# Turning the memory of a cross attention early, through a DRAM scratch, in a hybrid mLSTM/HGRN2 block

## The chip, the cores and the metric

The kernel runs on one core of a Trainium2 chip. The metric is the device time of one execution in microseconds, as a median of several runs. The core has five engines that matter here: TensorE (PE in the profile, its weight loads PEld), VectorE (DVE), ScalarE (ACT), GpSimd (POOL) and SyncE (SP), which issues most of the DMAs. Each engine takes its own instructions in the order in which the program lists them; semaphores make one wait for another.

## The reference

One block of a network in float32, batch 1, 256 tokens, width 2048: a feed-forward stage, a mixer of two recurrences, a cross attention over a memory of 256 rows, and a second feed-forward stage, each added to the residual stream.

```python
for l in range(DEPTH):
    h = rmsnorm(x, norm_ffn1[l])
    x = x + 0.5 * swiglu(h, ffn1_w1[l], ffn1_w3[l], ffn1_w2[l])
...
    h = rmsnorm(x, norm_xattn[l])
    m = rmsnorm(mem, norm_mem[l])
    x = x + cross_attention(h, m, xattn_wq[l], xattn_wkv[l], xattn_wo[l])
    h = rmsnorm(x, norm_ffn2[l])
    x = x + 0.5 * swiglu(h, ffn2_w1[l], ffn2_w3[l], ffn2_w2[l])
return rmsnorm(x, norm_final)
```

`mem` has 256 rows of 2048. Its norm divides each row by its root mean square and multiplies each column by `norm_mem`. `xattn_wkv` (2048 x 4096) then makes keys and values of four heads from it. The mixer is left out here, since the change does not touch it.

## The kernel before

**Gemms.** A matrix product has the activations as stationary operand and the weights streaming past. An activation of 256 rows is held turned: the 2048 columns lie on the partitions, in four chunks of 512 columns, each a tile of 128 x 4 x 256. Every float32 operand is split in two parts of lower precision, a high part (`oh` for activations, `wh` for weights) and the rest (`ol`, `wl`); a product is three matmuls, high by high (L269), high activation by low weight (L270) and low activation by high weight (L271).

A weight matrix is cut into units of four blocks of 128 rows by 512 columns, 1 MB, loaded by one DMA of SP into one of four raw buffers (`wr`). A unit is used in two pieces (four in the very first). For each piece `split` makes the high part with a copy on ScalarE (`wh`, L210) and the rest with a subtraction on VectorE (`wl`, L211); both have four buffers. A piece is twelve matmuls: two row blocks of weights, two halves of 128 tokens, three matmuls each.

**Order.** `run` goes through the pieces one after another: it emits loads for the pieces up to seven ahead, splits up to three ahead, then the matmuls of the piece, and calls `tick`. `tick` runs work that was put off: things due after a number of ticks (`after`), and a background list `self.bg`, from which it takes up to three items a tick as long as the estimated backlog of VectorE and ScalarE is under 2 us. The names `pa` are accumulators of gemms (four), `ps` other PSUM tiles (four). The framework's scheduler then places each engine's instructions, and may move them against the order of emission.

**First feed-forward stage.** For each of eleven columns of 512, a gemm with `ffn1_w1` (evicted by ScalarE with a Silu into `sil`) and one with `ffn1_w3` (multiplied into `sil` by VectorE, the "products"), eight pieces each. The products are then turned on VectorE: `turned` issues 16 transposes of 32 partitions by 256 elements, which turn every 32x32 block and put it at its place (`tt`); the copy `oh` and the rest `ol` follow.

**The memory.** After the first of four query gemms of the cross attention, `mem_prep` puts the memory's work into the background list: it loads four chunks of 256 x 512 (`mem`, two tiles of 128 rows each), sums their squares on ScalarE (`memss`), and turns them with `turn` on TensorE: a matmul with the identity for each block of 128 x 128 (L299), 32 in all, from where ScalarE and VectorE evict them as `oh` and `ol`, multiplied by `norm_mem`. The row factor `memr`, from the squares, is applied later, to keys and values. All tiles of 4 KB a partition (`mem`, `sil`, `tt`, `oh`, `ol` and others) share one pool `s4` of 22 buffers.

Instructions on VectorE and ScalarE pass through a small class that adds up their estimated time, so that all of them have line 90 in the profile; there one goes by the names of the tiles.

Of the kernel before, what the change touches and what calls it, by code (L numbers as in the profile page):

```python
# [12 lines left out]
F32 = mybir.dt.float32  # L13
F32R = mybir.dt.float32r
AF = mybir.ActivationFunctionType
ALU = mybir.AluOpType
# [3 lines left out]
P = 128  # L20
T = 256
D = 2048
# [39 lines left out]
class Sub:  # L62
    def __init__(self, unit, index, mm):
        self.unit, self.index, self.mm = unit, index, mm
        self.hi = self.lo = None
# [40 lines left out]
class Block:  # L106
# [4 lines left out]
    def __init__(self, ctx, tc, a, out):  # L111
        self.tc, self.nc, self.a, self.out = tc, Core(tc.nc), a, out
        pool = lambda name, bufs, **kw: ctx.enter_context(tc.tile_pool(name=name, bufs=bufs, **kw))
        self.const = pool("const", 1)
        self.xp = pool("xp", 1)
        self.wraw = pool("wraw", 4)
        self.whi = pool("whi", 4)
        self.wlo = pool("wlo", 4)
        self.s4 = pool("s4", 22)
        self.s2 = pool("s2", 4)  # L120
        self.small = pool("small", 4)
        self.acc = pool("acc", 4, space=PSUM)
        self.tr = pool("tr", 4, space=PSUM)
        self.steps = []
        self.now = 0
        self.pe = self.ready = 0.0
        self.unwritten = {}
        self.timed = []
        self.bg = deque()
        self.uid = 0  # L130
# [354 lines left out]
            if c < 3:  # L485
                self.load(units[c], parts=2 if c == 0 else 1)

    def rstd_of(self, ss, n, dim):
        nc = self.nc
        ms = self.sm(n, "ms")  # L490
        nc.vector.tensor_scalar(ms, ss, 1.0 / dim, EPS, op0=ALU.mult, op1=ALU.add)
        r = self.sm(n, "rstd", tag=f"rstd{n}")
        nc.gpsimd.tensor_tensor(r, ms, self.mhalf[:, :n], op=ALU.pow)
        nc.vector.end += 0.9
        return r
# [484 lines left out]
        return ths  # L980


    def mem_prep(self):
        nc = self.nc
        mem, self.memT = [None] * 4, [None] * 4
        ss = self.small.tile([P, 2, 4], F32, name="memss", tag="memss", bufs=1)

        def ld(c):
            mem[c] = self.t4([P, 2, 512], name="mem")
            nc.sync.dma_start(mem[c], self.a["mem"][0][:, c * 512:(c + 1) * 512].rearrange("(t p) n -> p t n", p=P))  # L990

        def sq(c):
            for t in range(2):
                self.squares(mem[c][:, t, :], ss[:, t, c:c + 1])
            if c == 3:
                s = self.sm(2, "mst")
                nc.vector.tensor_reduce(s, ss, axis=AX.X, op=ALU.add)
                self.memr = self.rstd_of(s, 2, D)

        def tn(c, half):  # L1000
            if half == 0:
                self.memT[c] = self.pair()
            self.turn(lambda t: mem[c][:, t, :], self.col["norm_mem"][:, 4 * c:4 * c + 4], self.memT[c], (half,))

        ths = [lambda: ld(0), lambda: ld(1)]
        for c in range(4):
            ths += [lambda c=c: sq(c), lambda c=c: tn(c, 0), lambda c=c: tn(c, 1)]
            if c < 2:
                ths.append(lambda c=c: ld(c + 2))
        return ths  # L1010
# [122 lines left out]
    def build(self):  # L1133
        nc, a = self.nc, self.a
        N = {}

        def begin(name):
            if name not in N:
                N[name] = self.norm_begin(name if name != "final" else None)
            return N[name]  # L1140
# [3 lines left out]
        def first(turn_gains):  # L1144
            self.warm(9)
            self.load_x()
            n = begin("norm_ffn1")
            n.ops = [self.pair() for _ in range(4)]
            src = lambda c: (lambda t: self.x[c][:, t, :])
            pin = self.tc.keep_in_program_order  # L1150
            turn_gains()
            first_subs = [st for st in self.steps if isinstance(st, Sub)][:4]
            for k in range(4):
                self.turn_piece(src(0), n.gain, n.ops[0], k, pin)
                if k == 0:
                    self.warm(4)
                self.split(first_subs[k])
            for i in range(2, 8):
                c, h = i // 2, i % 2
                fn = lambda c=c, h=h: self.turn(src(c), n.gain[:, 4 * c:4 * c + 4], n.ops[c], (h,), pin)  # L1160
                self.after((1, 2, 4, 5, 6, 7)[i - 2], fn)
            for c in range(4):
                self.after((5, 6, 8, 9)[c], lambda c=c: self.squares_of(n, c, pin=pin))
# [58 lines left out]
        n = len(self.steps)  # L1222
        self.steps.insert(n - 60, gains)
        first(turn_gains)
        self.run()


# [34 lines left out]
```

## Time and profile before

| | us |
|---|---|
| median of 3 runs (2537.36 to 2537.74) | 2537.58 |
| the profiled execution | 2537.33 |
| its span, first to last instruction | 2535.5 |
| TensorE busy | 2525.5 |
| VectorE busy | 1729.4 |
| ScalarE busy | 1209.6 |
| matmuls of 128 x 512 by each of the three lines, mean | 0.389 to 0.391 |
| low part of a weight piece, 128 x 1024, on VectorE, mean | 1.222 |
| high part of it on ScalarE, mean | 1.052 |
| weight load of 1 MB, from issue to landing, median | 5.2 |

In a row of the profile stand the line, the engine, the operation, the tiles as output<-inputs with their shapes, the count, then busy time and the mean of one, then how long the engine was idle just before these instructions and who ended that. A row of the timeline has the start and the length in microseconds first; several like instructions in a row are merged and counted. Matmuls overlap: the next starts before the one ahead has ended, so that the time between starts tells what one costs.

The span in forty slices of 63 us, the busy share of each in tenths. The first feed-forward stage fills the slices up to the eleventh:

```profile
PE   9999999999999999999999999999999999999998
...
DVE  6666644767768877867678787677766674457665
ACT  6444434444456566574444554444544443344443
```

### The profile page before, as it was taken

What the parts mean: (1) busy time and instruction counts of PE and PEld (TensorE: products, weight loads), DVE (VectorE), ACT (ScalarE), POOL (GpSimd) and SP (SyncE); (2) the same over time, 40 slices, a digit from 0 to 9 for tenths busy, and PEclk for the clock granted to TensorE, in tenths of its full rate; (3) what the DMA queues carried; (4) which work ended last, traced back from release to release, by engine and by line L of the source; (5) the groups of instructions that cost most, each with busy time, mean ns of one, the idle gap of its engine ahead of it and who ended that gap; (6) DMA issues with size and microseconds to landing.
All of it is one profiled execution on the core that took longest, in us unless ns stands there. A gap on an engine that the chain in (4) does not pass through costs nothing.

```text
span 2535.5 us, 29137 instructions
## 1 busy us (share of the span) xinstructions
PE 2525.5 (100%) x11463; PEld 2106.1 (83%) x11463; DVE 1729.4 (68%) x2372; ACT 1209.6 (48%) x1415; POOL 14.5 (1%) x21
## 2 busy tenths in 40 slices
PE   9999999999999999999999999999999999999998
PEld 7888888888888898888888888888888888888887
DVE  6666644767768877867678787677766674457665
ACT  6444434444456566574444554444544443344443
POOL 0000000000000000000000000000000000000000
PEclk9999999999999999999999999999999999999999
DMA  8566556565555545554655665555665655655653
GB/s 279 185 197 199 188 193 198 184 199 189 194 187 186 188 138 184 176 188 166 199 192 190 207 205 169 170 174 172 194 197 191 199 191 191 198 189 193 216 189 126
DMA packets 243593, 479.92 MB, mean 189 GB/s; under 512 B 8040, under 2 KB 14976, under 8 KB 243456
## 3 DMA queue, kind: packets, MB, share of 16 engines
q1 hardware_dynamic: 242992, 476.95, 58.0%
q8 instruction: 89, 1.46, 0.2%
q10 hardware_dynamic: 464, 1.12, 0.2%
q14 instruction: 48, 0.39, 0.0%
HBM read 475.94 MB, written 2.10 MB: 189 GB/s over the span
## 4 chain that ended last, share of the span: by engine, by line
PE 98%; DVE 0%; ACT 0%; issue 0%; DMA 0%; SPq 0%; POOLq 0%; POOL 0%; DVEq 0%; ACTq 0%
PE pa L270 32%; PE pa L269 32%; PE pa L271 32%; PE ps L783 1%; PE ps L1023 0%; PE ps L1024 0%; PE ps L1022 0%; PE ps L299 0%; DVE wl L90 0%; ACT wh L90 0%; DMA wr<-in_ffn_w 0%; ACT junk L90 0%; PE ps L1097 0%; DVE ol L90 0%; DVE x L90 0%
## 5 line engine op out<-in xcount | busy, mean ns | idle before, releaser
L90 DVE TENSOR_TENSOR wl<-wr,wh 128x1024 fp32r<-128x1024 f32 (+2 forms) x906 | 1093.8, 1211 | 701.7 <-ACT wh L90 694.2
L90 ACT CAST wh<-wr 128x1024 fp32r<-128x1024 f32 (+2 forms) x906 | 942.0, 1043 | 1121.8 <-PE pa L271 1075.6
L269 PE MATMUL pa<-wh,oh 128*128 128x512 f32 (+1 forms) x3614 | 1405.8, 389 | 0.1
L270 PE MATMUL pa<-wl,oh 128*128 128x512 f32 (+1 forms) x3614 | 1400.3, 388 | 0.2 <-DVE wl L90 0.2
L271 PE MATMUL pa<-wh,ol 128*128 128x512 f32 (+1 forms) x3614 | 1399.9, 387 | 0.0
L271 PEld LDWEIGHTS pa<-wh,ol 128*128 128x128 f32 x3614 | 678.3, 188 | 137.7
L270 PEld LDWEIGHTS pa<-wl,oh 128*128 128x128 f32 x3614 | 678.5, 188 | 136.4 <-DVE wl L90 1.5
L269 PEld LDWEIGHTS pa<-wh,oh 128*128 128x128 f32 x3614 | 678.3, 188 | 136.0 <-ACT wh L90 0.3
L90 DVE STREAM_TRANSPOSE tt<-sil 32x256 f32<-32x256 f32 x352 | 153.6, 436 | 6.8
L90 DVE STREAM_TRANSPOSE tt<-x 32x256 f32<-32x256 f32 x144 | 62.8, 436 | 2.8
L90 ACT CAST oh<-tt 128x1024 fp32r<-128x1024 f32 x29 | 30.6, 1056 | 41.2 <-DVE tt L90 41.2
L90 ACT ACT_TABLE_LOAD x35 | 44.9, 1283 | 8.2 <-DVE rs L90 2.7
L90 ACT ACTIVATE oh<-tt,cols 128x256 fp32r<-128x256 f32 x52 | 23.5, 501 | 42.8 <-DVE tt L90 42.8
L90 ACT ACTIVATE sil<-pa,rstd 128x512 f32<-128x512 f32 x44 | 29.8, 689 | 18.1 <-PE pa L271 18.0
L90 DVE TENSOR_TENSOR ol<-tt,oh 128x1024 fp32r<-128x1024 f32 x29 | 35.3, 1218 | 0.2 <-PE pa L270 0.2
L90 ACT ACTIVATE oh<-ps,cols 128x256 fp32r<-128x256 f32 x44 | 20.7, 472 | 26.0 <-DVE ol L90 22.1
L90 DVE STREAM_TRANSPOSE tt<-kn 32x256 f32<-32x256 f32 x64 | 27.9, 436 | 5.6 <-ACT kn L90 4.5
L90 DVE SCALAR_TENSOR_TENSOR sil<-pa,rstd,sil 128x512 f32<-128x512 f32 x44 | 31.0, 743 | 0.3 <-PE pa L271 0.3
L90 DVE STREAM_TRANSPOSE qt<-qn 32x256 f32<-32x256 f32 x64 | 27.9, 436 | 3.4 <-ACT qn L90 2.3
L90 DVE SCALAR_TENSOR_TENSOR ol<-ps,cols,oh 128x256 fp32r<-128x256 f32 x44 | 21.0, 480 | 11.6 <-ACT oh L90 11.6
L90 ACT ACTIVATE junk<-x 128x512 f32<-128x512 f32 (+1 forms) x41 | 25.0, 612 | 7.0 <-DVE x L90 7.0
L90 DVE COPY_PREDICATED at<-cst,ps 128x128 f32<-128x128 int32 x80 | 22.7, 328 | 6.9 <-PE ps L783 6.2
(189 smaller groups left out, 668.0 us busy)
## 6 DMA issues: line engine op xcount, KB each, us to landing
wr<-in_ffn_w SPq DMA_DIRECT2D x263, 1024.0 KB, 5.2
wr<-in_w_in SPq DMA_DIRECT2D x80, 1024.0 KB, 5.0
wr<-in_xattn_wkv SPq DMA_DIRECT2D x32, 1024.0 KB, 5.4
wr<-in_w_out SPq DMA_DIRECT2D x16, 1024.0 KB, 5.0
wr<-in_xattn_wq SPq DMA_DIRECT2D x16, 1024.0 KB, 5.1
wr<-in_xattn_wo SPq DMA_DIRECT2D x16, 1024.0 KB, 5.1
wr<-in_w_in SPq DMA_DIRECT2D x12, 688.0 KB, 4.0
wr<-in_w_proj_h SPq DMA_DIRECT2D x8, 1024.0 KB, 5.3
```

The source lines that it names most:

```text
L90: return fn(out, *args, **kw)
L269: nc.tensor.matmul(o, a_h, hi[:, j, :], start=(kt == 0), stop=False)
L270: nc.tensor.matmul(o, a_h, lo[:, j, :], start=False, stop=False)
L271: nc.tensor.matmul(o, a_l, hi[:, j, :], start=False, stop=(kt == end - 1))
L783: nc.tensor.matmul(ps[:, i, :], kt[:, g, j * P:(j + 1) * P], S["qc"][:, 2 * g + j, :], start=True, stop=True)
```

## The change

The memory's work is cut in two. `mem_early` is put into the background list after 24 ticks, in the first feed-forward stage. It loads the memory, sums the squares and computes `memr`, which gets a buffer of its own. Each chunk is turned within its 32x32 blocks by two transposes on VectorE of 128 x 512 (into `mu`), and stored with four DMAs of SP into a DRAM scratch `memD`, in such an order that it can be read back turned: each store takes 32 partitions, as 1024 runs of 32 elements (128 bytes). `mem_prep`, at its old place, loads the four chunks from the scratch (`memt`, one run of 1024 elements a partition) and makes `oh` and `ol` from them on ScalarE and VectorE. The 32 matmuls with the identity are gone.

```diff
@@
-    def rstd_of(self, ss, n, dim):
+    def rstd_of(self, ss, n, dim, **kw):
         nc = self.nc
         ms = self.sm(n, "ms")
         nc.vector.tensor_scalar(ms, ss, 1.0 / dim, EPS, op0=ALU.mult, op1=ALU.add)
-        r = self.sm(n, "rstd", tag=f"rstd{n}")
+        r = self.sm(n, "rstd", **(kw or {"tag": f"rstd{n}"}))
@@
-    def mem_prep(self):
+    def mem_early(self):
         nc = self.nc
-        mem, self.memT = [None] * 4, [None] * 4
+        mem = [None] * 4
         ss = self.small.tile([P, 2, 4], F32, name="memss", tag="memss", bufs=1)
+        self.memD = self.dram.tile([4, 32, 4, 8, 4, 32], F32, name="memD")
...
             if c == 3:
                 s = self.sm(2, "mst")
                 nc.vector.tensor_reduce(s, ss, axis=AX.X, op=ALU.add)
-                self.memr = self.rstd_of(s, 2, D)
-
-        def tn(c, half):
-            if half == 0:
-                self.memT[c] = self.pair()
-            self.turn(lambda t: mem[c][:, t, :], self.col["norm_mem"][:, 4 * c:4 * c + 4], self.memT[c], (half,))
+                self.memr = self.rstd_of(s, 2, D, tag="memr", bufs=1)
+
+        def tn(c):
+            u = self.t4([P, 4, 4, 2, 32], name="mu")
+            for t in range(2):
+                nc.vector.transpose(u[:, :, :, t, :].rearrange("p j k r -> p k j r"),
+                                    mem[c][:, t, :].rearrange("p (k j c) -> p k j c", k=4, j=4))
+            for i in range(4):
+                nc.sync.dma_start(self.memD[c][:, :, :, i, :].rearrange("c j e r -> c (j e) r"),
+                                  u[32 * i:32 * i + 32].rearrange("c j k t r -> c (j k t) r"))
 
         ths = [lambda: ld(0), lambda: ld(1)]
         for c in range(4):
-            ths += [lambda c=c: sq(c), lambda c=c: tn(c, 0), lambda c=c: tn(c, 1)]
+            ths += [lambda c=c: sq(c), lambda c=c: tn(c)]
+            if c < 2:
+                ths.append(lambda c=c: ld(c + 2))
+        return ths
+
+    def mem_prep(self):
+        nc = self.nc
+        mem, self.memT = [None] * 4, [None] * 4
+
+        def ld(c):
+            mem[c] = self.t4([P, 4, T], name="memt")
+            nc.sync.dma_start(mem[c].rearrange("p k t -> p (k t)"),
+                              self.memD[c].rearrange("c j e i r -> j c (e i r)"))
+
+        def parts(c):
+            self.memT[c] = hi, lo = self.pair()
+            self.unwritten.pop(id(self.memT[c]))
+            for k in range(4):
+                g = self.col["norm_mem"][:, 4 * c + k:4 * c + k + 1]
+                nc.scalar.activation(hi[:, k, :], mem[c][:, k, :], AF.Copy, scale=g)
+                nc.vector.scalar_tensor_tensor(lo[:, k, :], in0=mem[c][:, k, :], scalar=g,
+                                               in1=hi[:, k, :].bitcast(F32), op0=ALU.mult, op1=ALU.subtract)
...
@@ build
         first(turn_gains)
+        self.after(24, lambda: self.bg.extend(self.mem_early()))
         self.run()
```

The lines of the two kernels differ by one from L124 on, and by 34 at the end. How the scheduler places the early work is seen in the order of the built programs. The buffers' numbers differ between the two kernels; the raw tiles wr_714, wr_753, wr_787 and wr_821 of before hold the same weights as wr_726, wr_791, wr_849 and wr_883 now.

SP's queue in the second pair of gemms of the first stage, before:

```order
L198 DMA wr_678<-in_ffn_w 128x4x512
L198 DMA wr_714<-in_ffn_w 128x4x512
L198 DMA wr_753<-in_ffn_w 128x4x512
L198 DMA wr_787<-in_ffn_w 128x4x512
L198 DMA wr_821<-in_ffn_w 128x4x512
```

and now, where "x4" is four stores of one chunk:

```order
L199 DMA wr_680<-in_ffn_w 128x4x512
L994 DMA mem_718<-in_mem 128x2x512
L994 DMA mem_720<-in_mem 128x2x512
L199 DMA wr_726<-in_ffn_w 128x4x512
L1010 DMA memD<-mu_744 1024x1x32 x4
L994 DMA mem_751<-in_mem 128x2x512
L1010 DMA memD<-mu_778 1024x1x32 x4
L994 DMA mem_785<-in_mem 128x2x512
L199 DMA wr_791<-in_ffn_w 128x4x512
L1010 DMA memD<-mu_809 1024x1x32 x4
L1010 DMA memD<-mu_842 1024x1x32 x4
L199 DMA wr_849<-in_ffn_w 128x4x512
```

The load of wr_791 now stands behind the stores of the second chunk (mu_778), and that of wr_849 behind those of the third and the fourth (mu_809, mu_842).

VectorE around the products of the second pair (`sil` from `pa`), before. Pieces 33 to 37 of the kernel's gemms, counted from 0, have the low parts wl_806, wl_824, wl_840, wl_858 and wl_878; the products need the end of piece 33:

```order
L90 TENSOR_TENSOR wl_806<-wr_714,wh_805 128x1024
L90 TENSOR_TENSOR wl_824<-wr_753,wh_823 128x1024
L90 TENSOR_TENSOR wl_840<-wr_753,wh_839 128x1024
L90 TENSOR_TENSOR wl_858<-wr_787,wh_857 128x1024
L90 SCALAR_TENSOR_TENSOR sil_732<-pa_739,rstd_375,sil_732 128x512
L90 SCALAR_TENSOR_TENSOR sil_732<-pa_740,rstd_375,sil_732 128x512
L90 STREAM_TRANSPOSE tt_895<-sil_732 32x2x4x32
L90 TENSOR_TENSOR wl_878<-wr_787,wh_877 128x1024
```

and now, from the low part of piece 33 (wl_868) on:

```order
L90 TENSOR_TENSOR wl_868<-wr_726,wh_867 128x1024
L90 SCALAR_TENSOR_TENSOR sil_757<-pa_764,rstd_377,sil_757 128x512
L90 SCALAR_TENSOR_TENSOR sil_757<-pa_765,rstd_377,sil_757 128x512
L90 STREAM_TRANSPOSE mu_809<-mem_751 128x4x4x32 x2
L90 STREAM_TRANSPOSE mu_842<-mem_785 128x4x4x32 x2
L90 STREAM_TRANSPOSE tt_957<-sil_757 32x2x4x32
L90 TENSOR_REDUCE mst_820<-memss 128x2
L90 STREAM_TRANSPOSE tt_957<-sil_757 32x2x4x32
L90 TENSOR_SCALAR ms_822<-mst_820 128x2
L90 STREAM_TRANSPOSE tt_957<-sil_757 32x2x4x32 x7
```

followed by

```order
L90 TENSOR_TENSOR wl_886<-wr_791,wh_885 128x1024
L90 TENSOR_TENSOR wl_902<-wr_791,wh_901 128x1024
L90 STREAM_TRANSPOSE tt_957<-sil_757 32x2x4x32 x7
L90 TENSOR_TENSOR ol_938<-tt_957,oh_937 128x1024
L90 TENSOR_TENSOR wl_920<-wr_849,wh_919 128x1024
```

The low parts of pieces 34 to 36 (wl_886, wl_902, wl_920) stood ahead of the products and stand now behind them, behind two chunks of the memory, and behind nine (piece 34) or all sixteen (piece 36) of the transposes of the products. On TensorE the new order of piece 34 has two matmuls with the high part ahead of the first with the low part, where one stood.

More of the change, by code (lines that the diff above doesn't have):

```diff
@@ L123, in __init__ @@
         self.tr = pool("tr", 4, space=PSUM)
+        self.dram = pool("dram", 1, space=bass.MemoryType.DRAM)
         self.steps = []
@@ L997, in sq @@
                 nc.vector.tensor_reduce(s, ss, axis=AX.X, op=ALU.add)
-                self.memr = self.rstd_of(s, 2, D)
-        def tn(c, half):
-            if half == 0:
-                self.memT[c] = self.pair()
-            self.turn(lambda t: mem[c][:, t, :], self.col["norm_mem"][:, 4 * c:4 * c + 4], self.memT[c], (half,))
+                self.memr = self.rstd_of(s, 2, D, tag="memr", bufs=1)
[7 more added lines that the diff above has]
+                                  u[32 * i:32 * i + 32].rearrange("c j k t r -> c (j k t) r"))
         ths = [lambda: ld(0), lambda: ld(1)]
         for c in range(4):
-            ths += [lambda c=c: sq(c), lambda c=c: tn(c, 0), lambda c=c: tn(c, 1)]
+            ths += [lambda c=c: sq(c), lambda c=c: tn(c)]
[17 more added lines that the diff above has]
+                                               in1=hi[:, k, :].bitcast(F32), op0=ALU.mult, op1=ALU.subtract)
+        ths = [lambda: ld(0), lambda: ld(1)]
+        for c in range(4):
+            ths.append(lambda c=c: parts(c))
             if c < 2:
```

## The prediction

> **What bounds the kernel now.** I read the page first: the span, the busy times, the slices and the chain.
>
> ```profile
> span 2535.5 us, 29137 instructions
> PE 2525.5 (100%) x11463; PEld 2106.1 (83%) x11463; DVE 1729.4 (68%) x2372; ACT 1209.6 (48%) x1415; POOL 14.5 (1%) x21
> ...
> PE 98%; DVE 0%; ACT 0%; issue 0%; DMA 0%; SPq 0%; POOLq 0%; POOL 0%; DVEq 0%; ACTq 0%
> ```
>
> TensorE is never without work: it is busy for 2525.5 of 2535.5 us and makes 98% of the chain. So a change gains what it takes off TensorE, and loses what TensorE then has to wait. Next the waits, of TensorE and of SP's queue.
>
> ```profile
> PE pa L270 <- DVE wl L90: 0.2, 1, 0.2
> ...
> SPq L198 <- DVE wl L90: 2080.3, 410, 9.5
> ```
>
> TensorE waits for a split weight tile once, for 0.2 us; SP, which loads the weights, sits almost all the time at a wait for a free buffer. There is room, but it is held by the order in which SP and VectorE work: both take their instructions one after another.
>
> **What goes: 32 turns on TensorE.** The memory's turns, and TensorE around two groups of them:
>
> ```profile
> L299 PE MATMUL ps<-cst,mem x32: 270/272/273, 1465.0 to 1514.9; 128*128 128x128 f32 x32
> ```
>
> ```profile
> 1459.80 0.39 PE L270 MATMUL pa<-wl,oh 128*128 128x512 f32 x1
> ...
> 1462.52 0.39 PE L270 MATMUL pa<-wl,oh 128*128 128x512 f32 x1
> ...
> 1465.02 0.60 PE L299 MATMUL ps<-cst,mem 128*128 128x128 f32 x4
> 1465.37 0.48 PE L269 MATMUL pa<-wh,oh 128*128 128x512 f32 x1
> ...
> 1468.23 0.60 PE L299 MATMUL ps<-cst,mem 128*128 128x128 f32 x4
> ```
>
> Their durations overlap, so starts count. Undisturbed, twelve matmuls go from 1459.80 to 1462.52: 2.72 us, 0.227 each. From one group of four turns to the next, 1465.02 to 1468.23, lie the four and twelve matmuls: 3.21 us. A group costs 0.49, the eight groups 3.9 us. The evictions (16 on ScalarE, 16 on VectorE) stay, from SBUF now; the eight squares and the row statistics move to the first stage. TensorE doesn't wait here now, so no more than **3.9 us** is to be had.
>
> **What comes, and where it lies.**
>
> ```profile
> L90 ACT ACTIVATE kn<-pa,rstd x8: 688/690/690, 1541.8 to 1692.5; 128x512 f32<-128x512 f32 x8
> ```
>
> Eight turns on VectorE, eight squares on ScalarE and 16 stores, four loads come into the second pair of gemms of the first feed-forward stage; the four loads back stand in the cross attention where four loads of the same size stood, and I cost them at nothing: the first key product is evicted at 1541.8, so its gemm of eight pieces starts near 1520, 49 us after the last such load goes out now (1471.2, in the row of mem loads below). VectorE is idle for 32% of the span by the page, which would hide all of the early work; the order does not let it. A gemm piece is twelve matmuls, 2.72 us, and the split runs at most four pieces ahead. I number the pieces from 0; piece 34 is the first of the third pair (wl_824 before, wl_886 now), piece 36 the one with wl_858 and wl_920.
>
> ```profile
> 92.68 1.23 DVE L90 TENSOR_TENSOR wl<-wr,wh 128x1024 fp32r<-128x1024 f32 x1 [1.49 <-ACT wh L90]
> ...
> 99.26 1.40 DVE L90 SCALAR_TENSOR_TENSOR sil<-pa,rstd,sil 128x512 f32<-128x512 f32 x2
> 100.70 0.43 DVE L90 STREAM_TRANSPOSE tt<-sil 32x256 f32<-32x256 f32 x1
> ...
> 105.34 2.23 DVE L90 STREAM_TRANSPOSE tt<-sil 32x256 f32<-32x256 f32 x5
> ...
> 112.86 1.23 DVE L90 TENSOR_TENSOR wl<-wr,wh 128x1024 fp32r<-128x1024 f32 x1
> 114.01 1.22 DVE L90 TENSOR_TENSOR ol<-tt,oh 128x1024 fp32r<-128x1024 f32 x1
> ```
>
> ```profile
> 99.78 0.39 PE L270 MATMUL pa<-wl,oh 128*128 128x512 f32 x1
> ```
>
> ```profile
> 105.22 0.39 PE L270 MATMUL pa<-wl,oh 128*128 128x512 f32 x1
> ```
>
> Before, VectorE writes the low part of piece 34 at 92.68, six microseconds before the products at 99.26, which wait for the end of piece 33. Now that low part stands behind those products, behind four memory turns and behind nine turns of the products. TensorE, which needs it at 99.78, is made to wait for all of that: piece 33, products, turns, split, piece 34, one after another. What each takes:
>
> ```profile
> L90 DVE TENSOR_TENSOR suf<-suf,pre 128x512 f32<-128x512 f32 x14 | 9.7, 689 | 1.5 <-ACT pre L90 1.4
> L90 DVE TENSOR_TENSOR at<-ps,cst 128x256 f32<-128x256 f32 x8 | 3.4, 434 | 1.7 <-PE ps L783 1.7
> L90 DVE STREAM_TRANSPOSE tt<-sil 32x256 f32<-32x256 f32 x352 | 153.6, 436 | 6.8
> ```
>
> ```profile
> 112.87 1.06 ACT L90 CAST oh<-tt 128x1024 fp32r<-128x1024 f32 x1 [1.18 <-DVE tt L90]
> ```
>
> ```profile
> L90 DVE TENSOR_REDUCE mst<-memss x1: 161/161/161, 1489.2 to 1489.2; 128x2 f32<-128x8 f32 x1
> L90 DVE TENSOR_SCALAR ms<-mst x1: 168/168/168, 1489.4 to 1489.4; 128x2 f32<-128x2 f32 x1
> ```
>
> A turn of 128x512 isn't in the trace. One of 32x256 takes 436 ns, as 256 elements a partition take in a sum (434), so I take 0.70 for 512 (689 in a sum, and a gap). Its ends are 0.44 (no more than the 32x256) and 3.5 (32x32 blocks one by one, 64 for 8); the 689 is nearest. Then: products done and next start 100.70; four memory turns 2.8, 103.5; nine turns at 2.23/5, 4.0, and the two small ones 0.35: 107.85; low part 1.22: **109.1**. TensorE goes on there.
>
> The second wait follows: low part of piece 35 until 110.2 (1.15 after the last, as 112.86 to 114.01), seven turns 3.1 to 113.35, the high part of the turned products on ScalarE 1.06 to 114.4 (VectorE's next instruction waits for it), their low part 1.22 to 115.65, wl_920 1.2 to **116.9**. TensorE, from 109.1, would be there at 114.5 (24 matmuls of 0.227); in the old run it is there at 105.22, or 105.45 in the new order with two high-part matmuls ahead. All later work moves by 116.9 - 105.45 = **11.45 us**. After that the split catches up (1.2 a piece against 2.72), and nothing gives the delay back.
>
> SP must not be later than this. Its load for pieces 34 and 35 (wr_791) stands behind the stores of the second chunk, that for 36 and 37 (wr_849) behind those of the third and fourth.
>
> ```profile
> wr<-in_ffn_w SPq DMA_DIRECT2D x263, 1024.0 KB, 5.2
> ...
> mem<-in_mem SPq DMA_DIRECT2D x4, 512.0 KB, 6.0
> ```
>
> ```profile
> L990 SPq DMA_DIRECT2D mem<-in_mem x4: 463/500/501, 1449.0 to 1471.2; - x4
> ```
>
> ```profile
> 87.24 1.22 DVE L90 TENSOR_TENSOR wl<-wr,wh 128x1024 fp32r<-128x1024 f32 x1 [1.50 <-ACT wh L90]
> ```
>
> The second chunk is turned behind the low part of 87.24: 88.5 to 89.9. Four stores at 0.5 us of SP, a memory load, the weights at 92.4: landed by 97.6, by 100.5 with the stores' own time ahead; the split needs them at 106.8. The memory load, too, lands before its turn at 102.1. The other eight stores go out from 102.1 to 106.1, wr_849 at 106.1: landed at 111.3, at 113.2 with the stores' time. Needed at 114.4: **covered by 1.2 us**, if a store's packet is cheap. A store has 1024 packets of 128 bytes, 64 for each of 16 engines. No such packet is in the trace; two windows of SP's queue, with 16-byte packets alone and with stores of 1024 bytes, bound it:
>
> ```profile
> DMA packets 58, 0.00 MB, mean 2 GB/s; under 512 B 58, under 2 KB 58, under 8 KB 58
> ...
> q1 hardware_dynamic: 58, 0.00, 4.7%
> ```
>
> ```profile
> DMA packets 319, 0.33 MB, mean 271 GB/s; under 512 B 32, under 2 KB 288, under 8 KB 319
> ...
> q1 hardware_dynamic: 319, 0.33, 77.8%
> ```
>
> The first window is 0.55 us: 0.047 x 16 x 0.55 / 58 = 7 ns of an engine, and 9.5 ns apart on the queue as a whole. The second is 1.2 us: 0.778 x 16 x 1.2 / 319 = 47 ns. Between the two by bytes, 128 give 11.5 ns, which I take, as 16 is the nearer row: the eight stores are 8 x 64 x 11.5 = 5.9 us of an engine. From 14 ns on the weights land last.
>
> ScalarE's part, and TensorE's clock:
>
> ```profile
> 91.59 1.05 ACT L90 CAST wh<-wr 128x1024 fp32r<-128x1024 f32 x1 [1.67 <-PE pa L271]
> ```
>
> ```profile
> L90 ACT ACTIVATE junk<-mem x8: 617/632/665, 1456.3 to 1478.2; 128x512 f32<-128x512 f32 x8
> L90 ACT ACTIVATION_READ_ACCUMULATOR junk<-mem x8: 186/188/224, 1456.8 to 1478.7; 128x1 f32 x8
> ```
>
> ```profile
> 2527.00:2530.80 3.80, 0.00 (x0) 0.00 (x0) 2.54 (x9) 2.14 (x6) 0.66 (x1) 1.00 0.51 190
> 2530.80:2535.00 4.20, 0.00 (x0) 0.00 (x0) 0.15 (x1) 0.00 (x0) 0.00 (x0) 0.50 0.68 250
> ```
>
> ScalarE waits 1.67 us in every piece for TensorE; a square is 0.63 and 0.19, and the four late ones are over before VectorE's nine turns are, so they cost nothing. After the last matmul the granted clock stays at 1.00 for 3.8 us and is 0.50 from then on. The wait up to 109.1 is some 8 us, so TensorE may come back at half speed. If that lasts as long, it costs half of 3.8, 1.9 us, and arrives at piece 36 at 116.4 instead of 114.5: still before 116.9, so nothing. The Trainium skill (TensorE: Matmul & The Clock Gate, Part 1: The HAM clock gate) puts the change at an idle or busy window of about 3.4 us; the rows above agree for the way down.
>
> **The sum.** Profiled execution 2537.33 (span 2535.5 and 1.8 around it), 0.25 under the median of 2537.58. 2537.33 - 3.9 + 11.45 = 2544.9, as a median **2545.1**, slower by 0.3%. With turns of 0.44: 2544; with stores at 47 ns: below.
>
> **The rivals.**
> Dear stores. At 47 ns a chunk's four stores take 12 us of an engine: they end at 103.1, the memory load behind them lands at 105.7 instead of before 102.1 (3.6 later), the eight stores take 24 us from 107.1 to 131.1, wr_849 lands at 135.1, TensorE has piece 36 at 137.4: 32 us late, 2565.7. For it: a load has to go through the same queue behind them. Against: the 16-byte row. The Trainium skill (DMA: Bandwidth & Descriptors, Specifications) says that below 512 bytes the engine reads, modifies and writes; no run here shows it yet. Twice the 11.5 ns for that would be, as an estimate by this page, 2549.5.
> A queue that can't make packets faster than 9.5 ns each: a store 9.7 us, twelve of them in the two waits 117, together some 113 late: 2647. Against: 319 packets in 1.2 us are 3.8 ns apart.
> Other side: the cover holds. All added work fits into the idle time of VectorE, wl_886 is there when piece 33 ends, as wl_824 was; then only the 3.9 are left: 2533.7, faster. It decides at one point: the low part of piece 34 would have to be done before 99.78. Against it stands the row order: products that need the end of piece 33 stand ahead of it.
> The turns cost TensorE more than I read: matmul and weight load one after another, 0.272 and 0.140, for 32 are 13.2; then 2535.8, no difference. Against: the starts above.
>
> ```profile
> L299 PEld LDWEIGHTS ps<-cst,mem x32: 138/140/143, 1464.8 to 1514.8; 128*128 128x128 f32 x32
> ```
>
> The change may also not do what it says (the memory still turned on TensorE); the row order has no such matmul left, so I give it nothing.
>
> **Chances.** Forecast (2543 to 2547) 0.55; dear stores (2547 to 2566) 0.27; slow queue 0.06; cover holds 0.07; dear turns 0.05. The low end is the cheap turn less a microsecond, the high end the 47 ns; that holds 0.82. A measurement of this kernel tells some 0.2% (5 us) from no change: faster 0.07, same 0.05, slower 0.88.
>
> **What would show it.** In the profile after: no matmul at the cross attention's line 299 with mem, and there 3.9 us less; one wait of TensorE for wl of some 9 us near 100 us, a second of 2 near 115 (longer, and for a weight load, if stores are dear); a granted clock under 1 for some microseconds behind the first; turns of 128x512 near 0.7. I am wrong if TensorE doesn't wait there, or waits anywhere else.

## The result, and the profile after

| | us |
|---|---|
| median before (5 runs, 2537.36 to 2537.74) | 2537.6 |
| median after (5 runs, 2554.29 to 2556.6) | 2555.4 |
| ratio, 95% interval | 1.007, 1.006 to 1.0081 |
| profiled execution after, its span | 2556.6, 2554.8 |

The change makes the kernel 17.8 us slower; the forecast was 7.6 slower, with 2566 as the upper end. Of all executions reported here one, of pool_st at 2594.19 us, was slow, with a granted clock of 0.926 where the others have 0.99 or more; the ratios leave it out. The page of the changed kernel first: span, busy times, and the shares of the chain that ended last, by engine.

```profile
span 2554.8 us, 29095 instructions
...
PE 2530.5 (99%) x11431; PEld 2107.7 (82%) x11431; DVE 1733.6 (68%) x2380; ACT 1209.1 (47%) x1415; POOL 13.6 (1%) x21
...
PE 96%; DMA 1%; DVE 1%; ACT 1%; issue 0%; SPq 0%; POOLq 0%; POOL 0%; ACTq 0%; DVEq 0%
```

TensorE has 32 matmuls fewer (11431 against 11463), so the turns are gone, yet it is busy for 5.0 us more, and DMA, VectorE and ScalarE have each a per cent of the chain that TensorE had. Now TensorE's waits (who, for whom, us in total, times, longest):

```profile
PE pa L271 <- DVE wl L90: 7.9, 6, 5.5
...
PE pa L270 <- ACT wh L90: 5.7, 4, 2.4
```

Ten waits for split weights, where there was one. To see where, I compared the start of every gemm matmul (`pa`, 10854 of them in both kernels) with that of the same matmul before. This table gives, for each stretch of the program, by how many microseconds the kernel loses on the old one; it serves for all runs below.

| kernel | first gemm's start | pieces up to 36 of the first stage | cross attention, turns and readback | all the rest |
|---|---|---|---|---|
| changed | +1.9 | +12.8 | +3.7 | +0.6 |
| read16 | +0.3 | +15.4 | -3.7 | +0.5 |
| early_only | +0.2 | +12.6 | 0.0 | +0.3 |
| late_4 | +0.2 | 0.0 | +3.7 | +0.6 |
| spread | +1.6 | 0.0 | +2.2 | +0.4 |
| spread16 | +0.5 | 0.0 | -3.7 | +0.4 |
| turns_only | +0.3 | 0.0 | 0.0 | +0.6 |
| stores_only | +0.3 | +13.6 | 0.0 | +0.5 |
| pool_st | +0.1 | 0.0 | 0.0 | +0.5 |
| pinned | +0.4 | +9.7 | 0.0 | +0.5 |
| pool16 | +0.2 | 0.0 | -3.7 | +0.6 |
| read2 | +0.5 | 0.0 | +24.9 | +0.5 |

The changed kernel loses in two places. **First stage.** TensorE's matmuls with an idle time ahead of them, in the timeline from 100 to 126 us:

```profile
104.04 0.73 PE L270 MATMUL pa<-wh,oh 128*128 128x512 f32 x2 [2.41 <-ACT wh L90]
110.31 0.80 PE L271 MATMUL pa<-wl,oh 128*128 128x512 f32 x1 [5.54 <-DVE wl L90]
118.71 0.73 PE L270 MATMUL pa<-wh,oh 128*128 128x512 f32 x2 [0.48 <-ACT wh L90]
119.97 0.50 PE L271 MATMUL pa<-wl,oh 128*128 128x512 f32 x1 [0.53 <-DVE wl L90]
```

Piece 34's first matmul with the low part comes at 110.31 where it came at 99.78. VectorE and ScalarE there:

```profile
100.99 1.43 DVE L90 SCALAR_TENSOR_TENSOR sil<-pa,rstd,sil 128x512 f32<-128x512 f32 x2 [7.09 <-PE pa L272]
102.34 2.48 DVE L90 STREAM_TRANSPOSE mu<-mem 128x512 f32<-128x512 f32 x4
...
109.03 2.36 DVE L90 TENSOR_TENSOR wl<-wr,wh 128x1024 fp32r<-128x1024 f32 x2
...
115.68 1.23 DVE L90 TENSOR_TENSOR ol<-tt,oh 128x1024 fp32r<-128x1024 f32 x1 [1.11 <-ACT oh L90]
```

```profile
114.60 1.04 ACT L90 CAST oh<-tt 128x1024 fp32r<-128x1024 f32 x1 [9.67 <-DVE tt L90]
117.61 2.00 ACT L90 CAST wh<-wr 128x1024 fp32r<-128x1024 f32 x2 [1.97 <-DMA wr<-in_ffn_w]
```

The reader sees VectorE stand idle for 7.09 us for the end of piece 33, with the low part of piece 34 behind the products. Later ScalarE, free at 115.64, gets the weights of piece 36 (wr_849) only at 117.61.

The weights of pieces 34 and 35 (wr_791) come late too. In the timelines from 84 us on, VectorE's turns of the second memory chunk, SP's queue, and ScalarE's copies:

```profile
90.30 1.30 DVE L90 STREAM_TRANSPOSE mu<-mem 128x512 f32<-128x512 f32 x2
...
91.62 2.92 SPq L1010 DMA_DIRECT2D memD<-mu  x4
...
95.60 0.73 SPq L199 DMA_DIRECT2D wr<-in_ffn_w  x1
...
102.94 1.99 ACT L90 CAST wh<-wr 128x1024 fp32r<-128x1024 f32 x2 [1.57 <-DMA wr<-in_ffn_w]
```

The stores stand in SP's queue until VectorE has turned their chunk, and this load behind them goes out at 95.60, where the load of the same weights went out at 74.95 before. TensorE's wait of 2.41 us is for the copies at 102.94. With VectorE free, the low part could have followed at some 105.2 (an estimate: 102.94, the copy's 1.05 and the subtraction's 1.22), 3.5 us late once the later start of 1.9 is taken off. So the order of the splits is not the whole of the first loss.

**Cross attention.** ScalarE's high parts of the memory read back, in the timeline from 1476 to 1501 us, and a window of 3.0 to 3.6 us in each of three loads (window, then PE, PEld, DVE, ACT, POOL busy, granted clock, DMA share, GB/s):

```profile
1476.73 1.71 ACT L90 ACTIVATE oh<-memt,cols 128x256 fp32r<-128x256 f32 x4 [6.24 <-DMA memt<-memD]
1481.88 1.71 ACT L90 ACTIVATE oh<-memt,cols 128x256 fp32r<-128x256 f32 x4 [2.49 <-DMA memt<-memD]
1491.14 0.91 ACT L90 ACTIVATE oh<-memt,cols 128x256 fp32r<-128x256 f32 x2 [5.68 <-DMA memt<-memD]
...
1499.04 1.71 ACT L90 ACTIVATE oh<-memt,cols 128x256 fp32r<-128x256 f32 x4 [1.45 <-DMA memt<-memD]
```

```profile
1477.00:1480.00 3.00, 3.00 (x15) 2.49 (x14) 2.27 (x5) 2.38 (x5) 0.00 (x0) 1.00 0.26 104
...
1486.20:1489.40 3.20, 3.20 (x16) 2.63 (x15) 3.14 (x7) 0.00 (x0) 0.00 (x0) 1.00 0.26 102
1493.20:1496.80 3.60, 2.84 (x8) 2.04 (x9) 3.60 (x6) 3.60 (x7) 0.00 (x0) 0.75 0.25 97
```

```profile
1484.57 0.50 PE L270 MATMUL pa<-wh,oh 128*128 128x512 f32 x1 [1.09 <-ACT wh L90]
...
1493.04 0.50 PE L270 MATMUL pa<-wh,oh 128*128 128x512 f32 x1 [1.70 <-ACT wh L90]
```

ScalarE stands 15.9 us in all (6.24 + 2.49 + 5.68 + 1.45) for four loads of 512 KB. The weights' copies `wh` stand behind it, and TensorE, in the last fence, waits for those. TensorE's waits there come to 4.5 us, and from 1494.9 to 1498.5 its granted clock is 0.53, which costs some 1.7 more (0.47 x 3.6). While such a load runs alone, a quarter of the DMA engines' time is used: four of sixteen. The source of that load is written "j c (e i r)", and j is 4.

### The profile page after: what moved, and what is told of

Its sections match the earlier page's. It is cut to its first block, busy times and chain, and to the rows that moved or that the text cites. A ratio compares the mean times of both kernels' runs of the same rounds, so it can differ in the third digit from the quotient of the medians.

```text
span 2554.8 us, 29095 instructions
## 1 busy us (share of the span) xinstructions
PE 2530.5 (99%) x11431; PEld 2107.7 (82%) x11431; DVE 1733.6 (68%) x2380; ACT 1209.1 (47%) x1415; POOL 13.6 (1%) x21
## 4 chain that ended last, share of the span: by engine, by line
PE 96%; DMA 1%; DVE 1%; ACT 1%; issue 0%; SPq 0%; POOLq 0%; POOL 0%; ACTq 0%; DVEq 0%
PE pa L271 31%; PE pa L272 31%; PE pa L270 31%; PE ps L784 1%; DMA memt<-memD 1%; DVE wl L90 0%; ACT wh L90 0%; PE ps L1056 0%; PE ps L1057 0%; PE ps L1055 0%; DMA wr<-in_ffn_w 0%; SPq L1010 0%; DMA stage<-in_norm_ffn 0%; PE ps L300 0%; ACT junk L90 0%
## 5 line engine op out<-in xcount | busy, mean ns | idle before, releaser
L90 DVE SCALAR_TENSOR_TENSOR ol<-tt,cols,oh 128x256 fp32r<-128x256 f32 x52 | 22.7, 480 | 5.8 <-ACT oh L90 5.8
L90 DVE SCALAR_TENSOR_TENSOR x<-pa,x 128x512 f32<-128x512 f32 (+1 forms) x34 | 21.4, 667 | 3.2 <-PE pa L272 3.1
```

The lines of the kernel that those rows point to most:

```text
L90: return fn(out, *args, **kw)
```

## The experiments

The theory after the result: two separate stalls. In the first stage the order in which VectorE and ScalarE make the split parts; in the cross attention loads that run on four DMA engines. Rivals: the readback is slow because of what is done with it, or because the scratch was written in small packets; the first stage loses by the turns themselves, or by the packets of the stores. All runs are against the same kernel before, whose median was 2537.6 to 2537.7 in every set.

### read16: the readback on all engines

```diff
-            nc.sync.dma_start(mem[c].rearrange("p k t -> p (k t)"),
-                              self.memD[c].rearrange("c j e i r -> j c (e i r)"))
+            for j in range(4):
+                nc.sync.dma_start(mem[c][32 * j:32 * j + 32].rearrange("p k t -> p (k t)"),
+                                  self.memD[c][:, j].rearrange("c e i r -> c (e i r)"))
```

> Only the readback changes: each of the four loads of 128 rows is cut in four loads of 32 rows (the first dimension of the source is then 32 long instead of 4). Theory (a load whose source has a first dimension of 4 runs on 4 of the 16 DMA engines, lands some 6 us late and holds up the weights queued behind it): the cross attention's net +4.2 us becomes -3.9, so about 2547.3 us (2545 to 2549.5), and ScalarE's wait for the readback falls from 15.9 us to under 4. Rival (the stall comes from what is done with the readback on ScalarE and VectorE, or from reading a scratch that was written in pieces of 128 bytes): 2553 to 2557.

Measured: 2548.48 us (2547.58 to 2550.34), ratio 1.0043 (1.0029 to 1.0057). The cross attention goes from +3.7 to -3.7, and ScalarE no longer waits for the loads: the view of the tile `memt` has none in its list of who waited. The median falls by 6.9 us with the form of four loads alone. The first stage of read16 lost more than that of the changed kernel, 15.4 for 12.8: there the weights of piece 36 landed at 116.91, 8.1 us after they went out (7.1 in the changed kernel). Why they took longer was not tried.

### early_only: the early part without the readback

`mem_early` stays as in the change; `mem_prep` is that of the kernel before, with loads, squares and 32 turns with the identity.

```diff
-            ths.append(lambda c=c: parts(c))
+            ths += [lambda c=c: sq(c), lambda c=c: tn(c, 0), lambda c=c: tn(c, 1)]
```

> The early part as in the change (its scratch is written and never read), then the memory's old preparation with 32 turns on TensorE at its old place. Theory (the two losses are separate): the first stage loses the 12.8 us of the changed kernel (11.5 by the recorded step) and the cross attention loses nothing, so 2550.4 us; 2552.3 if the first gemm's start 1.9 us later belongs to the change. Rival (part of the loss in the first stage comes from how the whole program is placed, not from the early part): under 2546.

Measured: 2550.76 us (2550.52 to 2552.74), 1.0054 (1.0042 to 1.0067): the first stage loses 12.6, the cross attention nothing. The two losses are separate, and the later start of the first gemm isn't bound to the early part.

### late_4: the readback without the scratch

This kernel leaves out the turns and the stores and reads the memory as it lies. So the memory isn't turned and the result is not the block's; only the time is of use.

```diff
-        self.memD = self.dram.tile([4, 32, 4, 8, 4, 32], F32, name="memD")
+        self.memD = self.a["mem"][0].rearrange("r n -> (r n)").rearrange("(c p x) -> c p x", c=4, x=1024)
...
-            ths += [lambda c=c: sq(c), lambda c=c: tn(c)]
+            ths += [lambda c=c: sq(c)]
...
-                              self.memD[c].rearrange("c j e i r -> j c (e i r)"))
+                              self.memD[c].rearrange("(c j) x -> j c x", j=4))
```

> The early part keeps its loads and squares and drops turns and stores; the readback takes the same shape of load (128 rows of 1024 elements with a first dimension of 4) straight from the memory as it lies, so that the turning is left out of the computation. Theory: no stall in the first stage, +4.2 us net in the cross attention as in the changed kernel, so about 2541.8 us. Rival (the scratch, written in pieces of 128 bytes, is what reads slowly): the loads land as the weights do and the turns saved count in full, 2533.7.

Measured: 2541.78 us (2540.25 to 2543.92), 1.0016 (1.0008 to 1.0025); +3.7 in the cross attention and nothing in the first stage. ScalarE waits as long for a source that was never written in pieces (the view of the tile `memt`, who waited for which load, us and times):

```profile
  DMA memt<-in_mem: 17.9, 4
```

So neither the scratch nor its small packets make the readback slow.

### read2: the same loads on two engines

```diff
+            for j in (0, 2):
+                nc.sync.dma_start(mem[c][32 * j:32 * j + 64].rearrange("p k t -> p (k t)"),
+                                  self.memD[c][:, j:j + 2].rearrange("c j e i r -> j c (e i r)"))
```

with the early part as in spread, below.

> As spread, but each load of the readback is cut in two whose first dimension is 2 long. Theory (the length of the first dimension sets how many DMA engines serve a load): each load now runs on 2 of 16 engines and takes about 10 us alone where that of 4 takes 5, ScalarE's wait for the readback grows beyond 16.4 us to 30 or more, and the time from 2541.7 to between 2546 and 2562. Rival (more and smaller loads land sooner, which is what helped when they were cut in four): 2541.7 or less.

Measured: 2562.74 us (2562.3 to 2563.2), 1.0098 (1.0082 to 1.0113), a little above the range expected. Windows of it, and the wait:

```profile
1456.00:1459.00 3.00, 3.00 (x15) 2.49 (x14) 2.90 (x6) 1.33 (x2) 0.00 (x0) 1.00 0.13 48
...
1490.00:1494.00 4.00, 1.64 (x8) 1.02 (x6) 0.00 (x0) 0.00 (x0) 0.00 (x0) 1.00 0.13 51
```

```profile
  DMA memt<-memD: 38.3, 4
```

DMA share 0.13, two of sixteen, and half the GB/s. Smaller and more loads don't help by themselves; the first dimension decides. The Trainium skill (DMA: Bandwidth & Descriptors, Why a DMA increments its semaphore by 16 and not by 1) says it: the number of engines is the largest up to 16 that divides the slowest dimension, other than 1, of both access patterns. The shares 0.25 for 4 and 0.13 for 2 agree.

### spread: the early part at quiet ticks

```diff
-        ths = [lambda: ld(0), lambda: ld(1)]
...
+            self.after(38 + 16 * c, lambda c=c: ld(c))
+            self.after(42 + 16 * c, lambda c=c: sq(c))
+            self.after(43 + 16 * c, lambda c=c: tn(c))
```

> The early part is put at fixed ticks instead of the background list: chunk c is loaded at tick 38+16c, squared at 42+16c, turned and stored at 43+16c, where VectorE is busy for 0.9 to 1.6 of a piece's 2.7 us. The readback stays as in the change. Theory (VectorE's queue between product and split, and 16 stores in a row, made the two waits): at most 1 us is lost in the first stage, the +4.2 of the cross attention stays, so about 2541.8 us (to 2544.5 with the later start). Rival (1024 runs of 128 bytes a store delay the weights behind them wherever they stand): 2546 or more, with TensorE's waits behind a DMA at four places.

Measured: 2541.69 us (2540.16 to 2543.39), 1.0016 (1.0007 to 1.0025). No loss in the first stage with the same eight turns and 16 stores on the same queues: their place decides.

### turns_only, stores_only, pool_st: what moves the low parts

All three are early_only with one edit.

```diff
-            for i in range(4):
-                nc.sync.dma_start(self.memD[c][:, :, :, i, :].rearrange("c j e r -> c (j e) r"),
-                                  u[32 * i:32 * i + 32].rearrange("c j k t r -> c (j k t) r"))
```

> As early_only, without the 16 stores: the memory is loaded early, squared and turned on VectorE, and the turned tiles are not used; the old preparation follows later. Theory (the scheduler reckons with a weight that lands late behind the stores on SP's queue, and therefore puts its low part behind the product; without the stores that order does not arise): VectorE's queue keeps the low parts wl ahead of the product, no wait in the first stage, 2537.6 us (to 2539.5 with the later start). Rival (the eight turns of 0.67 us themselves are in the way, as the recorded step had it): 2545 to 2549.

```diff
-            for t in range(2):
-                nc.vector.transpose(u[:, :, :, t, :].rearrange("p j k r -> p k j r"),
-                                    mem[c][:, t, :].rearrange("p (k j c) -> p k j c", k=4, j=4))
...
-                                  u[32 * i:32 * i + 32].rearrange("c j k t r -> c (j k t) r"))
+                                  mem[c][32 * i:32 * i + 32].rearrange("p t (m r) -> p (t m) r", r=32))
```

> As early_only, without the eight turns: the 16 stores of the same shape take the memory's tiles as they were loaded, so that none waits for VectorE. Theory (the order): VectorE's queue now has the product (ends 100.5), 16 transposes of 0.45, the copy on ScalarE 1.04, ol 1.23 and only then the low part that piece 34 needs, ready at about 111.2 instead of 99.8: 11.4 us lost, 2549.0 us (2548 to 2552), though VectorE does less than in the changed kernel. Rival (the turns make the loss): under 2542.

```diff
-                nc.sync.dma_start(self.memD[c][:, :, :, i, :].rearrange("c j e r -> c (j e) r"),
+                nc.gpsimd.dma_start(self.memD[c][:, :, :, i, :].rearrange("c j e r -> c (j e) r"),
```

> As early_only, with the 16 stores issued by GpSimd, so that SP's queue holds weights alone. Theory (place on SP's queue, and the order that follows from it, cost; the packets do not): the low parts stand ahead of the product, under 1 us is lost, 2537.6 to 2540. Rival (16 times 1024 packets of 128 bytes delay the weights on the DMA engines, whoever issues them): a wait behind the weights near 110 us, 2541 or more.

Measured: turns_only 2538.44 us (2538.18 to 2540.05), 1.0004 (0.9995 to 1.0012); pool_st 2538.74 us (2538.55 to 2540.4 but for the one at 2594.19), 1.0004 (0.9995 to 1.0013); stores_only 2551.93 us (2551.02 to 2552.21), 1.0055 (1.0041 to 1.0069). The eight turns alone cost nothing that can be measured. Nor do turns and stores, when GpSimd issues the stores. The 16 stores on SP's queue cost it all, without a single turn. VectorE in turns_only has the low parts ahead of the products again, which need not wait:

```profile
98.42 1.22 DVE L90 TENSOR_TENSOR wl<-wr,wh 128x1024 fp32r<-128x1024 f32 x1 [1.50 <-ACT wh L90]
99.56 1.40 DVE L90 SCALAR_TENSOR_TENSOR sil<-pa,rstd,sil 128x512 f32<-128x512 f32 x2
```

VectorE, ScalarE, the load of the weights and two windows behind TensorE's wait in stores_only:

```profile
99.30 1.43 DVE L90 SCALAR_TENSOR_TENSOR sil<-pa,rstd,sil 128x512 f32<-128x512 f32 x2 [7.09 <-PE pa L272]
100.77 6.72 DVE L90 STREAM_TRANSPOSE tt<-sil 32x256 f32<-32x256 f32 x15
...
110.41 4.62 DVE L90 TENSOR_TENSOR wl<-wr,wh 128x1024 fp32r<-128x1024 f32 x4
```

```profile
108.19 1.04 ACT L90 CAST oh<-tt 128x1024 fp32r<-128x1024 f32 x1 [14.78 <-DVE tt L90]
109.14 3.88 ACT L90 CAST wh<-wr 128x1024 fp32r<-128x1024 f32 x4
```

```profile
84.92 0.72 SPq L199 DMA_DIRECT2D wr<-in_ffn_w  x1
```

```profile
110.30:113.70 3.40, 3.17 (x7) 2.08 (x8) 3.40 (x4) 2.72 (x3) 0.00 (x0) 0.50 0.00 0
113.70:116.50 2.80, 2.80 (x9) 2.20 (x8) 1.33 (x2) 0.20 (x1) 0.00 (x0) 0.58 0.89 266
```

The weights for pieces 34 and 35 went out at 84.92, 24 us ahead of their copy at 109.14. ScalarE was idle for 14.78 us: `oh` of the products stood in its queue ahead of `wh`. So here it is the order, not a late weight. My size was low, 11.4 for 13.6, for the most part since I had left out the clock: behind the wait it is granted at 0.50 and 0.58 (the last fence), which costs 0.50 x 3.4 + 0.42 x 2.8 = 2.9 us. That the scheduler moves the split parts because it reckons with late weights behind the stores fits all three runs, but its reckoning itself was not seen.

### pinned: the same queue of SP, another order

```diff
-        pin = self.tc.keep_in_program_order if self.now < 8 else lambda ins: ins
+        pin = self.tc.keep_in_program_order if self.now < 8 or 24 <= self.now < 48 else lambda ins: ins
```

> As early_only, with the same loads and stores in the same places of SP's queue, but the splits of the pieces made at ticks 24 to 47 keep their program order on ScalarE and VectorE. The low parts for pieces 34 and 35 then stand ahead of the product, the one for piece 36 still behind product, 16 transposes and ol (ready at about 111.2 where 105.45 is needed). Theory (the order on the two engines costs, not the landing of the weights): 5.7 us lost instead of 12.8, 2543.3 us (2542.5 to 2544.5), no wait at piece 34 and one at piece 36. Rival (the weights land late behind the stores, in whatever order they are split): a wait at piece 34 or 35 stays, 2548 to 2552.

Measured: 2548.02 us (2546.43 to 2548.15), 1.0039 (1.0027 to 1.0052). Half a miss. As the theory has it, there is no wait at piece 34 or 35 and one at 36. But 9.7 us are lost, not 5.7:

```profile
93.00 0.73 PE L270 MATMUL pa<-wh,oh 128*128 128x512 f32 x2 [1.10 <-ACT wh L90]
...
112.35 1.22 PE L270 MATMUL pa<-wh,oh 128*128 128x512 f32 x2 [4.65 <-ACT wh L90]
```

```profile
90.67 0.63 ACT L90 ACTIVATE junk<-mem 128x512 f32<-128x512 f32 x1 [4.31 <-DMA mem<-in_mem]
...
91.92 3.87 ACT L90 CAST wh<-wr 128x1024 fp32r<-128x1024 f32 x4
```

```profile
112.30:115.60 3.30, 3.02 (x6) 1.99 (x7) 3.30 (x4) 2.84 (x3) 0.00 (x0) 0.50 0.00 0
115.60:117.60 2.00, 2.00 (x7) 1.55 (x6) 1.55 (x2) 0.00 (x0) 0.00 (x0) 0.60 0.71 163
```

By the starts 2.2 us are lost at piece 31 and 7.5 at 36. In this order VectorE turns the second chunk at 77.97, not at 90.30, and the weights of pieces 34 and 35 go out at 85.39, not at 95.60: the order on VectorE also decides how long the stores hold up the weights behind them.

The loss at piece 31 is new: ScalarE's square of a memory chunk that lands late stands ahead of four copies of weights. And behind the wait at 112.35 the clock is 0.50 to 0.60 for 5.3 us. That is 2.5 us (half of 3.3, 0.4 of 2.0), with the wait 7.1 of the 7.5. Any load or product ahead of a split in those queues can hold it up.

### spread16 and pool16: both stalls mended

spread16 has the edits of spread and read16; pool16 those of pool_st and read16 on the changed kernel.

> Both mends at once: the early part at fixed ticks (chunk c loaded at 38+16c, squared at 42+16c, turned and stored at 43+16c) and each load of the readback cut in four of 32 rows. Theory (two separate stalls, in the first stage and at the readback, hide a gain of 3.9 us of TensorE's turns): no wait in either place, 2537.6 - 3.9 = 2533.7 us (to 2536 where the first gemm starts later). Rival (the turns' removal gives less, or the two mends disturb each other): 2537 or more.

> The changed kernel with two edits: the stores are issued by GpSimd, and each load of the readback is cut in four of 32 rows; the early part stays in the background list. Theory: as with both mends before, no wait in either place, 2533.7 to 2535. Rival (stores from GpSimd's queue have a price that the kernel without the readback did not show): 2536 or more.

Measured: spread16 2534.68 us (2534.59 to 2534.97), 0.9988 (0.998 to 0.9997); pool16 2534.9 us (2534.64 to 2535.19), 0.9989 (0.998 to 0.9998). Both beat the kernel before, by 3.0 and 2.7 us, with intervals that lie just under 1. TensorE's only wait for a split part in pool16 is the one that the kernel before had:

```profile
PE pa L271 <- DVE wl L90: 0.2, 1, 0.2
```

What was expected beyond that, a microsecond, is in the columns for the start and the rest.

## Why the prediction was right in part

**The gain, right.** 3.9 us for 32 turns. Where nothing else happens in the cross attention (read16, spread16, pool16) it is 3.7 by the starts, and 3.8 from pool_st to pool16 (2538.74 - 2534.9).

**The first wait, right in place and size.** TensorE waited 8.0 us (2.41 and 5.54) where I had some 9. The low part was to be ready at 109.1; it was at 110.2 (109.03 and half of 2.36), or 108.3 without the start that came 1.9 later. The memory turn estimated at 0.70 us took 0.67:

```profile
L90 DVE STREAM_TRANSPOSE mu<-mem x8: 668/669/704, 75.3 to 104.1; 128x512 f32<-128x512 f32 x8
```

What I put down to it was incomplete. I had the weights of pieces 34 and 35 landed by 100.5 at the latest and saw no wait for them; they landed at 102.94 (101.0 without the later start), and 2.41 of the 8.0 us are for their high part. That added nothing, since the low part came later still. I counted four memory turns into the path, 2.8 us, which is so; but the turns aren't why the low part stands there. stores_only puts it there with none. As the price of a wait I had 1.9 us of slow clock, absorbed; the clock did fall to half, and the second wait covered it here, as it did not in pinned:

```profile
110.20:113.80 3.60, 3.49 (x8) 2.82 (x9) 3.50 (x8) 0.00 (x0) 0.00 (x0) 0.50 0.95 162
113.80:117.00 3.20, 3.20 (x11) 2.46 (x10) 1.98 (x3) 1.04 (x1) 0.00 (x0) 0.66 1.03 377
```

**The second wait, mis-sized by a microsecond.** "Covered by 1.2 us" failed: wr_849 landed at 117.6, with the split ready for it at 115.64. TensorE's wait is only 1.0 us (0.48 and 0.53), because the slow clock had made it late itself. The price of a packet alone wasn't it. A window with the stores alone:

```profile
DMA packets 1644, 0.21 MB, mean 139 GB/s; under 512 B 1644, under 2 KB 1644, under 8 KB 1644
...
q1 hardware_dynamic: 1644, 0.21, 89.0%
```

In 1.5 us that is 0.89 x 16 x 1.5 / 1644 = 13.0 ns of an engine, where I took 11.5 and named 14 as the limit. The time that SP's queue took was:

```profile
103.66 6.76 SPq L1010 DMA_DIRECT2D memD<-mu  x8
110.51 10.94 SPq L199 DMA_DIRECT2D wr<-in_ffn_w  x5
```

Eight stores keep SP for 6.76 us, 0.85 each, where I had taken 0.5 from the memory loads. That is near the 0.83 us that the 64 packets of a store take on an engine (64 x 13.0 ns), so the packets may be what held SP; no run separates the two. The weights go out 6.85 us after the first store, not 4.0, and land 7.1 later, as I had it (106.1 to 113.2). With this the first stage lost 12.8 where 11.45 was forecast. The rival of dear stores, at 47 ns and 32 us, didn't come about; the 13.0 ns show no doubled price for a packet of 128 bytes, which the Trainium skill's note on reads and writes below 512 bytes (DMA: Bandwidth & Descriptors, Specifications) made me fear.

**The step that failed: the readback.** "The four loads back stand in the cross attention where four loads of the same size stood, and I cost them at nothing." I compared bytes and the date of need of the first key product, and missed two things. The load's source starts with a dimension of 4, and runs on four engines. And what waits for it is not the key product but ScalarE's queue, which has to make the weights' high parts of the query gemms behind it. That cost 7.4 us (from +3.7 to -3.7), and turned the gain of 3.7 into a loss of as much. By the prediction's own words I am wrong if TensorE waits anywhere else; it did.

**The start.** The first gemm began 1.9 us later in the profiled execution. TensorE waited for the gains of the first norm:

```profile
6.03 0.26 PE L418 MATMUL ps<-cst,stage 16*128 16x16 f32 x1 [0.77 <-DMA stage<-in_norm_ffn]
```

This matmul began at 5.10 before, so the wait accounts for 0.9. Behind it eight small matmuls (`ps<-warm`) and six turns of `x` take 1.91 and 1.49 us where they took 1.06 and 0.82, while the profile shows a granted clock of 1.00 in both kernels. The later start varies from 0.1 to 1.9 between the profiled executions of the runs, and the runs of the changed kernel lie 2.3 us apart, those of before 0.4 in the same set. Why the changed program's first loads vary more was not tried; it stays open.

The sum by the starts: 1.9 + 12.8 + 3.7 + 0.6 = 19.0 for the profiled executions (2556.6 - 2537.33 = 19.3). Predicted were 11.45 - 3.9 = 7.55. Of the difference of 11.5, 7.4 are the readback, 1.9 the start, 1.3 the first stage, 0.2 the turns and 0.6 the rest.

The measured 2555.4 lies in the stated range only by luck. The forecast proper was 2543 to 2547; the part above it was opened for dear stores, which did not come about, and the readback, costed at nothing, makes up most of the distance.

## What to carry to other kernels

Before costing a moved load at nothing, read the first dimension of both its ends (it can put 512 KB on four engines) and the queue of the engine that waits for it, since everything behind that wait is late too. Where a scheduler places instructions, a DMA in the queue of the weight loads can reorder engines that never touch it: compare the order with the DMA on another queue. A change that takes work off the bounding engine is worth its 3.8 us only where nothing that waits for the moved work stands ahead of a split, or ahead of a weight load in its queue.

## What was not expected of the hardware

- A load's DMA share follows the first dimension of its access pattern: 0.25 to 0.26 with 4 (some 100 GB/s), 0.13 with 2 (some 50).
- A store of 1024 runs of 128 bytes cost 13.0 ns of an engine for each packet, and in the changed kernel kept SP 0.85 us where eight followed each other; from GpSimd's queue the same stores did no measurable harm.
- After waits of 4.65 and 5.54 us TensorE's granted clock was 0.50 in the next 3.3 and 3.6 us, and 0.60 and 0.66 in the 2.0 and 3.2 behind that.
